# Gate and up tiles of the second feed-forward block: two tiles of eight K-tiles each as a 2x2x2 block product in seven multiplications

## The chip, the cores and the metric

The kernel runs on one core of a Trainium2 chip, as one launch. The metric is device time in microseconds (us); of the kernel before there are three runs, and their median counts. In the profile PE is TensorE's matmul, PEld its weight load, DVE is VectorE, ACT is ScalarE, POOL is GpSimd, and SP is the engine that issues the transfers.

## The reference

One layer of an encoder block for 512 tokens of width 1024, in float32: a half-step SwiGLU feed-forward block, a parallel token mixing (a sparse and a latent attention), and a second feed-forward block of the first one's form, then a last norm. The change is in the second feed-forward block:

```python
def swiglu(h, w_in, w_down):
    g, u = jnp.split(h @ w_in, 2, axis=-1)
    return (jax.nn.silu(g) * u) @ w_down
...
        h = modulate(rmsnorm(x, g_ffn2[l]), sh3, sc3)
        x = x + 0.5 * gt3[:, None, :] * swiglu(h, w_ffn2_in[l], w_ffn2_down[l])
    return rmsnorm(x, g_final)
```

w_ffn2_in is 1024 x 5632 (2816 gate columns, 2816 up columns), w_ffn2_down 2816 x 1024.

## The kernel before

Activations lie transposed, features on the 128 partitions and the 512 tokens along the free axis, so that weights are the stationary operand. A float32 operand is split on the chip into two float32r parts, hi and lo: ACT writes hi (a rounded copy), DVE or POOL writes lo = source - hi (`split`). A product is three matmuls into the same PSUM bank, hi*hi, hi*lo and lo*hi (`mm3`).

`swiglu` runs a feed-forward block. `first_group` makes the normalized and modulated input h K-tile by K-tile (8 K-tiles of 128 features, each with a hi and a lo part, `modulated`), and multiplies each at once, in halves of 256 tokens, with the weights of the first six output tiles: three gate and three up tiles. The other 19 gate tiles and 19 up tiles follow as pairs: for each pair two weight tiles of 512 KB are loaded and split (`weights`), and each is multiplied over the 8 K-tiles (`proj`) into a PSUM bank of its own. `gated` takes silu of the gate tile (ACT), multiplies it with the up tile (DVE, which reads PSUM), and splits the result into a hidden tile's two parts. The 22 hidden tiles come in thirds of 8, 7 and 7 (THIRDS); after each third, eight down tiles multiply its hidden tiles with w_ffn2_down and add to x. So pairs come in runs of 5, 7 and 7. In the last third the last four down tiles run in halves of 256 tokens, and each half's final norm follows as soon as it can.

The order of the work isn't written out. The block is traced into a list of operations (`Plan.record`), each with an estimated cost (`Plan.cost`), and a list scheduler (`Plan.order`) gives each engine its queue: of the operations that could start now, the one that was traced first. Each cost is estimated for the operation by itself. An operation starts when its operands are there and a buffer for its result is free. SBUF is 66 slots of 2 KB and 17 of 4 KB per partition (SLOTS); each kind of buffer has a limit (CAPS): one staging tile (wst), seven tiles each of weight parts (whi, wlo, 4 KB each). PSUM is eight banks, of which projections use six. The engines then work through their queues in order, and wait by semaphores where they must. All operations go through one recorded call, so every row of the profile has the line L602 of `issue`; rows are told apart by their tiles: f2h and f2l are the parts of h, wh_ and wl_ weight parts, ws_ staged weights, and of weight tiles _f is the first group's, _2g, _2u and _2d the gate, up and down tiles, hh and hl the hidden tiles' parts. Buffer numbers are left out.

POOL has no work in the second feed-forward block but clearing one half tile at its beginning.

Of the kernel before, what the change touches and what calls it, by code (L numbers as in the profile page):

```python
"""Hybrid streaming-encoder residual block: macaron SwiGLU, DSA + MLA token mixing, macaron SwiGLU.

Activations are kept transposed, features on the partitions and the 512 tokens along the free
axis, so that every projection has its weights stationary and streams N = 512 tokens. A float32
product runs as three passes of the tensor engine: each operand is split exactly into two
12-bit-significand parts (float32r) on the chip, and hi*hi + hi*lo + lo*hi accumulate in PSUM.
"""
# [17 lines left out]
P = 128  # L25
# [21 lines left out]
# the work up to the end of the first projections, in the order of its urgency, and what engines wait for  # L47
# [18 lines left out]
WG_POOL = (1, 3)  # L66
RING = 2
# [3 lines left out]
CAPS = {"x": 4, "x2": 8, "sq": 4, "h": 16, "hid": 20, "sg": 1, "mt0": 2, "mt256": 2, "nrm": 6, "wst": 1, "whi": 7, "wlo": 7,  # L71
# [5 lines left out]
# the mixing: I index scores, A sparse queries, L latents, U latent values, R rotary queries, P query and key  # L77
# pairs, S and W scores and values of a latent head, T top-k, G gates, D and E scores and values of four sparse heads
# [5 lines left out]
# its operations in the order of their urgency, and what engines wait for  # L84
# [29 lines left out]
TINY = {"norm": 16, "top1": 2, "top2": 2, "top3": 2, "mla": 24, "dsa": 24}  # L114
# [8 lines left out]
# columns of the packed per-feature vectors  # L123
V_BADA, V_G1, V_GM, V_G2, V_GF, V_GCQ, V_GCKV = 0, 72, 80, 88, 96, 104, 107
# constants and the T5 table in the same pack
# [3 lines left out]
def _mt(w):  # L129
    """(K, M) -> [M/128][128 partitions of K][K/128][128]"""  # L130
    k, m = w.shape
    return w.reshape(k // P, P, m // P, P).transpose(2, 1, 0, 3)


def _prep(inp):
# [45 lines left out]
    # rows that mask the first 64 queries of each block from its last 64 keys: queries, keys  # L181
# [12 lines left out]
# The block below is traced once into a list of operations on buffers without addresses. A list  # L194
# scheduler then orders them over the engines, each operation by its priority as soon as its operands
# and a slot for its result are there, and gives every buffer its slot; they are issued in that order.
# [5 lines left out]
class View:  # L202
# [31 lines left out]

    def bitcast(self, dt):
        return View(self.buf, self.chain + [("bitcast", dt)], self.p, self.off, self.dims, dt)
# [5 lines left out]
    def box(self):  # L242
        """partitions, columns, and the runs of columns where these have holes"""
# [11 lines left out]
    def real(self):  # L255
        ap = self.buf.base()
        for kind, *a in self.chain:
            if kind == "get":
                ap = ap[a[0]]
            elif kind == "bitcast":  # L260
                ap = ap.bitcast(a[0])
            else:
                ap = ap.rearrange(a[0], **a[1])
# [44 lines left out]
class Clock:  # L308
    """the tensor engine's clock: half as fast after a window in which it did little"""
# [21 lines left out]
# functions of ScalarE by the table that it loads for them  # L331
# [3 lines left out]
class Plan:  # L335
# [13 lines left out]
    # -- tracing  # L349
    @contextlib.contextmanager  # L350
    def after(self, op, everything=False):
        """loads, or all work, that is not to run ahead of an operation"""
# [10 lines left out]
    def record(self, eng, nc_engine, fn, args, kw):  # L363
# [14 lines left out]
        if op.eng == "pe":  # L378
            # the share of the time in which rows of the array work
# [16 lines left out]
        for v in outs:  # L396
# [9 lines left out]
            if eng == "pe":  # L406
                # a group's first matmul clears the flags of the whole bank: it comes after all matmuls
                # that were there before, and before all that follow; its last one after all of it
# [28 lines left out]
    def cost(eng, fn, outs, ins, kw, args):  # L437
        """an estimate, for the order alone"""
# [20 lines left out]
    # -- scheduling  # L459
    def order(self):  # L460
# [28 lines left out]
        while len(done) < len(self.ops):  # L489
            best = None  # L490
            for e, lst in ready.items():
# [4 lines left out]
                for op in lst:  # L496
# [4 lines left out]
                    for b in op.banks:  # L501
                        # a bank serves one engine at a time
# [9 lines left out]
                # an engine is not to begin something long just before urgent work  # L512
# [62 lines left out]
    def classes(b):  # L575
        """the kinds of slots that hold the buffer; a small one may take a large slot"""
        return (BANK,) if b.tag in BANK_CAPS else [c for c in SLOTS if c >= b.units]

    def take(self, b, live, s):
        """the slot that has been free for longest"""  # L580
# [24 lines left out]
class Block:  # L605
# [8 lines left out]
    def small(self, kind, n=4):  # L614
        """per-partition scalars, from a ring of its own for each kind of use"""
# [11 lines left out]
    def later(self):  # L627
        """work that only fills what the rest leaves free"""
# [5 lines left out]
    def urgent(self, *engines):  # L634
        """work that all of the next work waits for"""
# [4 lines left out]
    def split(self, hi, lo, src, engine=None):  # L640
        """hi + lo == src: hi rounded to float32r by ScalarE, the rest by VectorE"""
# [12 lines left out]
    def mm3(self, ps, wh, wl, xh, xl, start, stop, hh=True):  # L654
        mm = self.nc.tensor.matmul
        if hh:
            mm(ps, wh, xh, start=start, stop=False)
        mm(ps, wh, xl, start=False, stop=False)
        mm(ps, wl, xh, start=False, stop=stop)

    def proj(self, w, x, nk, name, tag, cols=ALL):
        """one tile of 128 output features: sum over nk K-tiles"""
# [8 lines left out]
    def squares(self, norm, t, cols=ALL, alone=False):  # L671
        """add a tile's squares to the sums of a norm, or keep them for the tensor engine to add"""
# [886 lines left out]
```

## Time and profile before

| | us |
|---|---|
| runs | 1180.87, 1183.2, 1185.97 |
| median of the runs | 1183.2 |
| span of the profiled execution, first to last instruction | 1182.4 |
| PE busy in it | 1137.4 |
| second block: from its first pair's first matmul to the last pair's end | 288.4 |

The page gives the profiled execution's span alone; what lies around it isn't told, so its own time is taken as the span. That lies within the three runs, 0.8 us below their median. In the profile, a row of a group gives its busy time, the mean of one in ns, and the idle time of its engine just before it with what ended it. Matmuls are pipelined: the record of one reaches over the beginning of the next, so the time that one costs is the distance of the starts.

### The profile page before, as it was taken

Reading aid. Unit: us, or ns where it says so; the run is one execution under the profiler, and the core shown is the slowest. Engines: PE = TensorE matmul, PEld = TensorE weight load, DVE = VectorE, ACT = ScalarE, POOL = GpSimd, SP = SyncE. Lnnn points to the kernel's source line nnn. Section 1 sums busy time; section 2 is a strip of 40 time slices with the busy share of each in tenths; the row PEclk is TensorE's granted clock in tenths of the full one; section 3 lists DMA queues with packets and bytes.
Section 4 is the critical chain, followed back from the end, with each engine's and each line's share of the span. In section 5 each row is a group of like instructions: output and inputs, shape, how many; then the busy total and the mean of one; then the engine's idle time right before and its main releaser. Section 6 shows DMA issues by size and latency. Waiting matters only on the chain. (4 is left out here: it accounts for less than half of the span.)

```text
span 1182.4 us, 15861 instructions
## 1 busy us (share of the span) xinstructions
PE 1137.4 (96%) x5955; PEld 949.1 (80%) x5957; DVE 744.1 (63%) x1381; ACT 502.6 (43%) x896; POOL 123.3 (10%) x111
## 2 busy tenths in 40 slices
PE   5999999999999999988999999999999999999996
PEld 3878788887877899776888777889988888888886
DVE  8876665547664796899997786848433333333335
ACT  5562413423343256454768777524432222223220
POOL 5120000000000000021235352000000000000000
PEclk8899999999999999999999999999999999999998
DMA  8555566548545753221144256423322332333212
GB/s 292 188 182 180 171 225 194 175 166 271 182 152 184 264 172 121 72 81 65 55 127 123 95 190 209 157 68 112 107 97 99 92 105 78 100 107 100 83 32 71
DMA packets 64543, 163.88 MB, mean 139 GB/s; under 512 B 9762, under 2 KB 21538, under 8 KB 64467
## 3 DMA queue, kind: packets, MB, share of 16 engines
q1 hardware_dynamic: 64466, 162.88, 41.7%
q8 instruction: 46, 0.75, 0.3%
q14 instruction: 31, 0.25, 0.1%
HBM read 148.11 MB, written 13.63 MB: 137 GB/s over the span
## 5 line engine op out<-in xcount | busy, mean ns | idle before, releaser
L602 DVE CUSTOM_DVE_ANT_0 junk<-ada,sc,vecs 128x1024 bf16<-128x1024 f32 x66 | 84.5, 1281 | 28.6 <-DMA ada<-in_w_ada_dram 28.4
L602 PE MATMUL bank<-hmh,wh_ib 128*128 128x512 f32 x200 | 79.8, 400 | 1.7 <-ACT wh_ib L602 1.7
L602 PE MATMUL bank<-hmh,wl_ib 128*128 128x512 f32 x200 | 80.2, 404 | 0.3 <-POOL wl_ib L602 0.3
L602 PE MATMUL bank<-hml,wh_ib 128*128 128x512 f32 x200 | 79.5, 398 | 0.0
L602 DVE TENSOR_TENSOR wl_2d<-ws_2d,wh_2d 128x896 fp32r<-128x896 f32 (+1 forms) x24 | 27.3, 1137 | 75.2 <-ACT wh_2d L602 75.2
L602 PE MATMUL bank<-hl,wh_2d 128*128 128x512 f32 (+1 forms) x204 | 73.6, 361 | 0.0
L602 PE MATMUL bank<-hh,wh_2d 128*128 128x512 f32 (+1 forms) x204 | 73.5, 360 | 0.0
L602 PE MATMUL bank<-hh,wl_2d 128*128 128x512 f32 (+1 forms) x204 | 73.4, 360 | 0.0
L602 PE MATMUL bank<-hh,wh_1d 128*128 128x512 f32 (+1 forms) x197 | 72.6, 369 | 0.0
L602 PE MATMUL bank<-hl,wh_1d 128*128 128x512 f32 (+1 forms) x197 | 72.4, 367 | 0.0
L602 PE MATMUL bank<-hh,wl_1d 128*128 128x512 f32 (+1 forms) x197 | 72.2, 366 | 0.0
L602 DVE TENSOR_TENSOR wl_2g<-ws_2g,wh_2g 128x1024 fp32r<-128x1024 f32 x19 | 23.3, 1225 | 60.1 <-ACT wh_2g L602 60.1
L602 DVE SCALAR_TENSOR_TENSOR x<-bank,gt,x 128x512 f32<-128x512 f32 (+1 forms) x66 | 44.0, 666 | 25.5 <-PE bank L602 25.4
L602 PE MATMUL bank<-f1h,wh_1g 128*128 128x512 f32 x152 | 59.5, 391 | 0.0
L602 PE MATMUL bank<-f1l,wh_1g 128*128 128x512 f32 x152 | 59.2, 389 | 0.0
L602 PE MATMUL bank<-f1h,wl_1g 128*128 128x512 f32 x152 | 59.2, 389 | 0.0
L602 PE MATMUL bank<-f2h,wh_2g 128*128 128x512 f32 x152 | 59.1, 389 | 0.0
L602 PE MATMUL bank<-f2l,wh_2g 128*128 128x512 f32 x152 | 59.1, 389 | 0.0
L602 PE MATMUL bank<-f1h,wh_1u 128*128 128x512 f32 x152 | 59.1, 389 | 0.0
L602 PE MATMUL bank<-f1l,wh_1u 128*128 128x512 f32 x152 | 59.1, 389 | 0.0
L602 PE MATMUL bank<-f2h,wl_2g 128*128 128x512 f32 x152 | 59.1, 389 | 0.0
L602 PE MATMUL bank<-f2h,wh_2u 128*128 128x512 f32 x152 | 59.1, 389 | 0.0
(328 smaller groups left out, 3088.2 us busy)
## 6 DMA issues: line engine op xcount, KB each, us to landing
ada<-in_w_ada_dram SPq DMA_DIRECT2D x72, 512.0 KB, 4.5
ws_ib<-in_wib_dram SPq DMA_DIRECT2D x25, 512.0 KB, 3.4
ws_1g<-in_w1b_dram SPq DMA_DIRECT2D x19, 512.0 KB, 3.7
ws_1u<-in_w1b_dram SPq DMA_DIRECT2D x19, 512.0 KB, 3.5
ws_2g<-in_w2b_dram SPq DMA_DIRECT2D x19, 512.0 KB, 3.7
ws_2u<-in_w2b_dram SPq DMA_DIRECT2D x19, 512.0 KB, 3.4
ws_1d<-in_w1d_dram SPq DMA_DIRECT2D x16, 448.0 KB, 3.5
ws_2d<-in_w2d_dram SPq DMA_DIRECT2D x16, 448.0 KB, 3.2
```

The source lines that it names most:

```text
L602: op.fn(*[real(v) for v in op.args], **{k: real(v) for k, v in op.kw.items()})
```

## The change

For a pair of a gate and an up tile, the K-tiles are taken in two halves (0 to 3, 4 to 7) and the tokens in two halves (a and b), so that the pair is a product of a 2x2 by a 2x2 matrix of blocks. It is made by seven block products in place of eight, each of 4 K-tiles and 256 tokens.

On the weights' side POOL makes four sums and differences of 128x512 per pair, and the parts of the staged gate tile (p0), of the combinations (p12, p34) and of half of the up tile (p22) are written; the lo part of p22 is POOL's. On the tokens' side four combinations are made for each of the four pairs of K-tiles k and k+4, once, in `token_combinations`; for that the modulated tiles are kept (m2), and `first_group` takes the K-tiles in the order 0, 4, 1, 5, 2, 6, 3, 7. In this group POOL writes the lo part of the weights of K-tiles 4, 5 and 6. On the output side the products accumulate in two PSUM banks, A and C: a product is added in PSUM to one whose value has been copied out before, and DVE adds the others, three times 256 columns and once 512. Loads of the pairs' weights wait for the matmuls of the third K-tile of the first group.

```diff
+W2_POOL = (4, 5, 6)
+FAST_FROM = 2
...
+CAPS = {"m2": 5, "fst": 3, "t2": 4, "th": 16, "wct": 3, "vhi": 2, "vlo": 2, "g4": 2, "sv": 2, "x": 4,
...
-    def modulated(self, h, x, r, a, sh, cols):
+    def modulated(self, h, x, r, a, sh, cols, kept=None):
         nc = self.nc
         hi, lo = (t[:, cols] for t in h)
-        t = self.g(f"m{h[0].name}_{cols.start}", shape=(P, cols.stop - cols.start), tag=f"mt{cols.start}")
+        t = kept[:, cols] if kept is not None else self.g(f"m{h[0].name}_{cols.start}", shape=(P, cols.stop - cols.start), tag=f"mt{cols.start}")
         nc.vector.scalar_tensor_tensor(t, x[:, cols], a, r[:, cols], op0=ALU.mult, op1=ALU.mult)
         nc.scalar.activation(hi, t, AF.Identity, bias=sh)
         nc.vector.scalar_tensor_tensor(lo, t, sh, hi.bitcast(F32), op0=ALU.add, op1=ALU.subtract)
 
-    def first_group(self, name, site, r, src, n, widths, before=None, w0=None):
+    def first_group(self, name, site, r, src, n, widths, before=None, w0=None, fast=None):
...
-        h = []
+        h = [None] * KD
...
-        for k in range(KD):
+        ks = [k // 2 + KD // 2 * (k % 2) for k in range(KD)] if fast is not None else list(range(KD))
+        kept = {}
+        for k in ks:
             with at(f"w{k}"):
                 wh, wl = w0 if w0 and not k else self.weights(
-                    src[k], f"{name}{k}", n, engine=nc.gpsimd if not site and k in W0_POOL else None)
+                    src[k], f"{name}{k}", n,
+                    engine=nc.gpsimd if not site and k in W0_POOL or fast is not None and k in W2_POOL else None)
             if before:
...
-            h.append(tuple(self.g(f"{name}{c}{k}", F32R, tag="h") for c in "hl"))
+            h[k] = tuple(self.g(f"{name}{c}{k}", F32R, tag="h") for c in "hl")
+            if fast is not None:
+                kept[k] = self.g(f"m{name}{k}", tag="m2")
...
                 with self.urgent() if k < URGENT else contextlib.nullcontext(), at(f"m{k}{i}"):
-                    self.modulated(h[k], self.x[k], r, a, sh, cols)
+                    self.modulated(h[k], self.x[k], r, a, sh, cols, kept.get(k))
                 with at(f"f{k}{i}"):
...
                         self.mm3(first[m][:w, cols], wh[:, c], wl[:, c], h[k][0][:, cols], h[k][1][:, cols],
-                                 False, k == KD - 1 and cols.stop == S, not start)
+                                 False, k == ks[-1] and cols.stop == S, not start)
+            if fast is not None and k == ks[FAST_FROM]:
+                self.fast_from = nc.last_pe
+            if fast is not None and k >= KD // 2:
+                fast.append(self.token_combinations(f"{name}t{k}", site, k - KD // 2, kept[k - KD // 2], kept[k]))
         return first, h
 
+    def token_combinations(self, name, site, k, m0, m1):
+        nc = self.nc
+        V = nc.vector
+        a, b = HALVES
+        sh = self.mod[:, site * 24 + k + KD // 2:site * 24 + k + KD // 2 + 1]
+        d = self.small("shift", 1)
+        V.tensor_tensor(d, sh, self.mod[:, site * 24 + k:site * 24 + k + 1], op=ALU.subtract)
+        t12, t34 = (self.g(f"{name}{i}", shape=(P, 2, S // 2), tag="t2") for i in (1, 3))
+        nc.gpsimd.tensor_tensor(t12[:, 0], m0[:, b], m0[:, a], op=ALU.subtract)
+        V.scalar_tensor_tensor(t34[:, 0], m1[:, b], d, m0[:, b], op0=ALU.add, op1=ALU.subtract)
+        V.scalar_tensor_tensor(t12[:, 1], m1[:, b], sh, t12[:, 0], op0=ALU.add, op1=ALU.subtract)
+        V.scalar_tensor_tensor(t34[:, 1], m1[:, a], sh, t12[:, 1], op0=ALU.add, op1=ALU.subtract)
+        out = []
+        for i, t in enumerate((t12, t34)):
+            hi, lo = (self.g(f"{name}{c}{i}", F32R, shape=(P, 2, S // 2), tag="th") for c in "hl")
+            self.split(hi, lo, t)
+            out += [(hi[:, e], lo[:, e]) for e in range(2)]
+        return out
+    def fast_pair(self, name, src0, src1, h, t):
+        nc = self.nc
+        V, G = nc.vector, nc.gpsimd
+        a, b = HALVES
+        half = S // 2
+        K4 = KD // 2
+        w0, w1 = (self.g(f"ws_{name}{i}", shape=(P, D), tag="fst") for i in range(2))
+        with nc.after(self.fast_from):
+            nc.sync.dma_start(w0, src0)
+            nc.sync.dma_start(w1, src1)
+        s12, s34 = (self.g(f"wc_{name}{i}", shape=(P, D), tag="wct") for i in range(2))
+        lo_, hi_ = slice(0, S), slice(S, D)
+        G.tensor_tensor(s12[:, hi_], w1[:, lo_], w1[:, hi_], op=ALU.add)
+        G.tensor_tensor(s12[:, lo_], s12[:, hi_], w0[:, lo_], op=ALU.subtract)
+        G.tensor_tensor(s34[:, lo_], w0[:, lo_], w1[:, lo_], op=ALU.subtract)
+        G.tensor_tensor(s34[:, hi_], w0[:, hi_], s12[:, lo_], op=ALU.subtract)
+        def parts(n, t, tag, w, engine=None):
+            hi = self.g(f"wh_{name}{n}", F32R, shape=(P, w), tag=tag + "hi")
+            lo = self.g(f"wl_{name}{n}", F32R, shape=(P, w), tag=tag + "lo")
+            self.split(hi, lo, t, engine)
+            return hi, lo
+        p0 = parts("a", w0, "w", D)
+        p12 = parts("s", s12, "w", D)
+        p34 = parts("t", s34, "w", D)
+        p22 = parts("b", w1[:, hi_], "v", S, G)
+        A, C = (self.bank(f"{n}_{name}", "mm") for n in "ac")
+        cols = lambda hs, at: [(hs[0][:, at + k * P:at + k * P + P], hs[1][:, at + k * P:at + k * P + P]) for k in range(K4)]
+        def product(ps, w, x, start=False):
+            for k in range(K4):
+                self.mm3(ps, *w[k], *x[k], start and k == 0, k == K4 - 1, skip_group_check=True)
+        quarter = lambda k0, c: [(h[k0 + k][0][:, c], h[k0 + k][1][:, c]) for k in range(K4)]
+        T = [[t[k][i] for k in range(K4)] for i in range(4)]
+        g = self.g(f"g_{name}", shape=(P, 4, half), tag="g4")
+        v = self.g(f"v_{name}", shape=(P, 2, half), tag="sv")
+        product(A[:, a], cols(p0, 0), quarter(0, a), True)
+        product(A[:, b], cols(p12, 0), T[1])
+        product(C[:, a], cols(p12, S), T[0], True)
+        product(C[:, b], cols(p34, 0), T[2])
+        nc.scalar.copy(v[:, 0], A[:, a])
+        V.tensor_tensor(v[:, 0], v[:, 0], A[:, b], op=ALU.add)
+        product(A[:, a], cols(p0, S), quarter(K4, a))
+        V.tensor_tensor(v[:, 1], v[:, 0], C[:, a], op=ALU.add)
+        V.tensor_tensor(g[:, 3], v[:, 1], C[:, b], op=ALU.add)
+        product(C[:, a], cols(p34, S), quarter(K4, b))
+        product(C[:, b], cols(p22, 0), T[3])
+        V.tensor_tensor(g[:, 1:3], v[:, 0].repeat(2), C.rearrange("p (e t) -> p e t", e=2), op=ALU.add)
+        return g, A[:, a]
...
     def swiglu(self, n, site, r, before_group=None, w0=None, fill=None, after_group=None):
         nc, A = self.nc, self.A
+        combos = [] if n == 2 else None
         first, h = self.first_group(f"f{n}", site, r, A[f"w{n}a"], 2 * FIRST * P, [P] * (2 * FIRST),
-                                    before_group, w0)
+                                    before_group, w0, combos)
         if after_group:
             after_group()
         hid = [None] * NP_FF
...
             gated(i, first[2 * i], first[2 * i + 1])
+        def gated_fast(i):
+            src = A[f"w{n}b"][i - FIRST]
+            g, c11 = self.fast_pair(f"f{i}", src[0], src[1], h, combos)
+            nc.scalar.activation(g[:, 0], c11, AF.Silu)
+            nc.scalar.activation(g[:, 1], g[:, 1], AF.Silu)
+            nc.vector.tensor_tensor(g[:, 0:2], g[:, 0:2], g[:, 2:4], op=ALU.mult)
+            hi, lo = self.g(f"hh{n}_{i}", F32R, tag="hid"), self.g(f"hl{n}_{i}", F32R, tag="hid")
+            e = lambda t: t.rearrange("p (e t) -> p e t", e=2)
+            nc.scalar.copy(e(hi), g[:, 0:2])
+            nc.vector.tensor_tensor(e(lo), g[:, 0:2], e(hi).bitcast(F32), op=ALU.subtract)
+            hid[i] = (hi, lo)
         for t, (i0, i1) in enumerate(THIRDS):
             for i in range(max(i0, FIRST), i1):
+                if n == 2:
+                    gated_fast(i)
+                    continue
                 pool = lambda e: nc.gpsimd if n == 1 and 2 * (i - FIRST) + e in WG_POOL else None
                 wg = self.weights(A[f"w{n}b"][i - FIRST, 0], f"{n}g{i}", engine=pool(0))
...
```

`View.repeat` makes a view that reads one tile twice; `mm3` hands `skip_group_check` on; comments and docstrings are left out of the new file.

## Rows read from the trace of the kernel before

**Rows 1.** The page: busy time of each engine, and POOL's tenths in 40 slices.

```profile
PE 1137.4 (96%) x5955; PEld 949.1 (80%) x5957; DVE 744.1 (63%) x1381; ACT 502.6 (43%) x896; POOL 123.3 (10%) x111
...
POOL 5120000000000000021235352000000000000000
```

**Rows 2.** Windows: length, busy us and instructions of PE, PEld, DVE, ACT, POOL; clock, DMA.

```profile
841.10:1129.50 288.40, 288.40 (x1275) 238.87 (x1274) 102.99 (x112) 80.62 (x97) 0.00 (x0) 1.00 0.29 95
797.00:841.00 44.00, 44.00 (x362) 43.60 (x361) 30.20 (x72) 19.51 (x31) 0.00 (x0) 1.00 0.36 111
```

**Rows 3.** Waits of PE from 805 to 1175 us: total, times, longest.

```profile
PE bank L602 <- DVE dg_n L602: 2.5, 1, 2.5
```

**Rows 4.** Timeline of PE, last pair: start us, duration us, operation.

```profile
1118.58 0.39 PE L602 MATMUL bank<-f2h,wh_2g 128*128 128x512 f32 x1
...
1124.02 0.39 PE L602 MATMUL bank<-f2h,wh_2u 128*128 128x512 f32 x1
...
1129.46 0.39 PE L602 MATMUL bank<-hh,wh_2d 128*128 128x512 f32 x1
```

**Rows 5.** Timeline of PE, last down tiles in halves: first matmul of each half.

```profile
1148.50 0.28 PE L602 MATMUL bank<-hh,wh_2d 128*128 128x256 f32 x1
...
1158.57 0.28 PE L602 MATMUL bank<-hh,wh_2d 128*128 128x256 f32 x1
```

**Rows 6.** Windows, within those halves.

```profile
1149.00:1160.00 11.00, 11.00 (x94) 11.00 (x93) 4.62 (x10) 2.30 (x5) 0.00 (x0) 1.00 0.01 1
```

**Rows 7.** Timelines, POOL (two rows) and DVE (two rows): starts of operations in succession.

```profile
702.03 1.29 POOL L602 TENSOR_TENSOR bt<-bt,mask 128x512 f32<-128x512 f32 x1
703.28 0.45 POOL L602 TENSOR_TENSOR oal<-osA,oah 64x128 fp32r<-64x128 f32 x1
...
822.45 1.22 DVE L602 TENSOR_TENSOR wl_2g<-ws_2g,wh_2g 128x1024 fp32r<-128x1024 f32 x1
823.58 0.88 DVE L602 SCALAR_TENSOR_TENSOR f2l<-mf2h,mod,f2h 128x256 fp32r<-128x256 f32 x2
```

**Rows 8.** Groups of DVE by shape: busy us, mean ns, idle before.

```profile
L602 DVE TENSOR_TENSOR hl<-sg,hh 128x512 fp32r<-128x512 f32 x44 | 30.4, 691 | 22.4 <-ACT hh L602 22.4
...
L602 DVE TENSOR_TENSOR wl_2g<-ws_2g,wh_2g 128x1024 fp32r<-128x1024 f32 x19 | 23.3, 1225 | 60.1 <-ACT wh_2g L602 60.1
...
L602 DVE SCALAR_TENSOR_TENSOR f2l<-mf2h,mod,f2h 128x256 fp32r<-128x256 f32 x16 | 7.3, 482 | 1.6 <-ACT f2h L602 1.6
...
L602 DVE TENSOR_TENSOR acc_n<-acc_n,sq_n 128x256 f32<-128x256 f32 x17 | 7.3, 427 | 2.6 <-ACT sq_n L602 2.3
```

**Rows 9.** Groups of ACT by shape.

```profile
L602 ACT CAST wh_2g<-ws_2g 128x1024 fp32r<-128x1024 f32 x19 | 19.9, 1050 | 57.0 <-DMA ws_2g<-in_w2b_dram 57.0
```

**Rows 10.** Timelines, DVE and POOL side by side: two meetings.

```profile
57.73 0.75 DVE L602 SCALAR_TENSOR_TENSOR f1l<-mf1h,mod,f1h 128x512 fp32r<-128x512 f32 x1
58.39 0.74 DVE L602 SCALAR_TENSOR_TENSOR mf1h<-x,a,bank 128x512 f32<-128x512 f32 x1
57.84 2.88 POOL L602 TENSOR_TENSOR adap<-ada,sc 128x1024 f32<-128x1024 f32 x1 [4.72 <-DVE wl_f L602]
...
503.43 0.69 DVE L602 TENSOR_TENSOR cql<-lat,cqh 128x512 fp32r<-128x512 f32 x1
504.43 2.49 DVE L602 TENSOR_TENSOR cql<-lat,cqh 128x512 fp32r<-128x512 f32 x1
504.00 2.38 POOL L602 TENSOR_TENSOR wl_ib<-ws_ib,wh_ib 128x1024 fp32r<-128x1024 f32 x1 [8.69 <-ACT wh_ib L602]
```

**Rows 11.** Timeline of DVE, first group: the second half's norm arrives.

```profile
814.21 0.87 DVE L602 SCALAR_TENSOR_TENSOR mf2h<-x,a,bank 128x256 f32<-128x256 f32 x2 [0.59 <-PE bank L602]
```

**Rows 12.** Groups of POOL by shape.

```profile
L602 POOL TENSOR_TENSOR bt<-bt,mask 128x256 f32<-128x256 f32 x8 | 6.4, 804 | 6.2 <-DVE osB L602 5.2 <-DVE mask L602 0.6 <-DMA bt<-bias 0.4
...
L602 POOL TENSOR_TENSOR wl_f<-ws_f,wh_f 128x768 fp32r<-128x768 f32 x2 | 4.3, 2128 | 13.1 <-DVE mod L602 7.9 <-ACT wh_f L602 5.2
```

More of the change, by code (lines that the diff above doesn't have):

```diff
@@ L70 @@
 SLOTS = {1: 66, 2: 17}
-CAPS = {"x": 4, "x2": 8, "sq": 4, "h": 16, "hid": 20, "sg": 1, "mt0": 2, "mt256": 2, "nrm": 6, "wst": 1, "whi": 7, "wlo": 7,
+CAPS = {"m2": 5, "fst": 3, "t2": 4, "th": 16, "wct": 3, "vhi": 2, "vlo": 2, "g4": 2, "sv": 2, "x": 4, "x2": 8, "sq": 4, "h": 16, "hid": 20, "sg": 1, "mt0": 2, "mt256": 2, "nrm": 6, "wst": 1, "whi": 7, "wlo": 7,
         "ust": 2, "uhi": 3, "ulo": 2, "ada": 3, "junk": 1, "adap": 2, "zero": 1, "dn": 1, "mr": 1, "sc": 2, "t5m": 8, "t5o": 2, "t5i": 2, "t5d": 1,
@@ L113 @@
 """
-TINY = {"norm": 16, "top1": 2, "top2": 2, "top3": 2, "mla": 24, "dsa": 24}
+TINY = {"norm": 16, "shift": 4, "top1": 2, "top2": 2, "top3": 2, "mla": 24, "dsa": 24}
 BANK_CAPS = {"mm": 6, "rn": 2, "t5": 2, "ix": 2, "mg": 3, "uk": 1, "sa": 3, "sb": 3, "tpa": 2, "tpb": 1,
@@ L233, in rearrange, with repeat @@
         return View(self.buf, self.chain + [("rearrange", pat, kw)], self.p, self.off, dims, self.dt)
+    def repeat(self, n):
+        return View(self.buf, self.chain + [("repeat", n)], self.p, self.off, [(0, n)] + self.dims, self.dt)
     def bitcast(self, dt):
@@ L261, in real @@
                 ap = ap.bitcast(a[0])
+            elif kind == "repeat":
+                ap = ap.unsqueeze(1)
+                ap = ap.broadcast_to([ap.shape[0], a[0], *ap.shape[2:]])
             else:
@@ L652, in weights, with mm3 @@
         return hi, lo
-    def mm3(self, ps, wh, wl, xh, xl, start, stop, hh=True):
+    def mm3(self, ps, wh, wl, xh, xl, start, stop, hh=True, **kw):
         mm = self.nc.tensor.matmul
         if hh:
-            mm(ps, wh, xh, start=start, stop=False)
-        mm(ps, wh, xl, start=False, stop=False)
-        mm(ps, wl, xh, start=False, stop=stop)
+            mm(ps, wh, xh, start=start, stop=False, **kw)
+        mm(ps, wh, xl, start=False, stop=False, **kw)
+        mm(ps, wl, xh, start=False, stop=stop, **kw)
     def proj(self, w, x, nk, name, tag, cols=ALL):
```

## The prediction, made before the changed kernel ran

> **What bounds the kernel now.** I read the page's shares first: TensorE (PE) is busy for 1137.4 of 1182.4 us, GpSimd (POOL) for 10% of it, and by the slices POOL does next to nothing in the last 40% of the span [rows 1]. Then the table by stage: in the second feed-forward block's 288.4 us of gate, up and down tiles PE is busy without a gap at granted clock 1.00 (the 2.4 GHz level), VectorE (DVE) for 103.0 and ScalarE (ACT) for 80.6 us, POOL for nothing, and the DMA share is 0.29 [rows 2]. Last, PE's waits from 805 us to the end: the longest is 2.5 us, on the last norm, outside that stretch [rows 3]. So here PE sets the time alone: 19 pairs of gate and up tiles, and 16 of the 24 down tiles. A microsecond of matmul taken out counts in full, as long as the others keep feeding PE.
>
> **Matmuls.** A pair is 2 tiles x 8 K-tiles x 3 passes = 48 matmuls of 512 tokens; from 1118.58 to 1129.46 they took 10.88 us, 226.7 ns each [rows 4]. 19 pairs are 206.7 us. The change makes of a pair 7 products x 4 K-tiles x 3 passes = 84 matmuls of 256 tokens. The trace holds this form: the first halves of the last four down tiles are 4 x 7 x 3 = 84 such matmuls with a new weight each, and took 1158.57 - 1148.50 = 10.07 us, 119.9 ns each [rows 5]. It is not the 7/8 that the columns promise, since 2 x 119.9 is 6% over 226.7; the weight loads are busy for 11.00 of 11.00 us there [rows 6]. Per pair 0.81 us goes, over 19 pairs **15.4 us**. Both terms come from the same shapes, so I give them no width.
>
> A rule of the Trainium skill speaks against this: "TensorE: Matmul & The Clock Gate", section The mechanism, has a weight load overlap a running matmul only when their row groups differ, and these fill all rows. With that page's load time of 107 ns and its 107 ns for 256 columns a matmul would take about 214 ns (an estimate from that page) and a pair 18 us. The 119.9 ns of rows 5, for the same form, decide against it.
>
> **First group.** Its 288 matmuls stay, only the K order changes (0, 4, 1, 5, ...). I cost that at nothing: PE is busy through 797 to 841 us [rows 2], and DVE, at 30.2 of 44.0 us, is the cover; what DVE gets in addition is in the next part.
>
> **What feeds the pairs.** Per pair POOL gets five 128x512 operations with two SBUF inputs (four weight combinations, one lo part). One takes 1.25 us from start to start [rows 7], so 6.25 us. DVE gets three lo parts of 128x1024 instead of two (record 1.225 us [rows 8]; records overlap the next by 0.09 [rows 7], so 1.13), the gate product and the hidden lo part (0.60 each), and four additions that read PSUM (3 x 0.34 + 0.60): 3.39 + 1.20 + 1.62 = 6.2 us. ACT gets three 1.05 us conversions [rows 9] and about 2.4 us of smaller work: 5.6 us. Taken singly, all lie under PE's 10.07. Loads stay two of 512 KB per pair.
>
> Taken together they don't, and this is the part that decides. DVE operations with two SBUF inputs and POOL operations don't run side by side here: a DVE subtraction of 128x512 began at 504.43 and took 2.49 us where it needs 0.69, and ended 0.54 after the POOL operation of 504.00 to 506.38; a POOL operation beginning at 57.84 took 2.88 instead of some 2.4 behind a DVE operation; a DVE operation with a PSUM input, at 58.39, ran in its usual 0.74 beside it [rows 10]. The pair's shared claim is POOL 6.25 + DVE 3.39 + 1.20 = **10.84 us**, against 10.07 for PE. What carries it is that the pairs come in runs of 5, 7 and 7, with eight down tiles between, in which POOL has nothing to do and DVE one lo part per tile. The 17 large slots hold a pair's six weight parts and the next pair's staging and combinations, so I count one pair prepared ahead of the second and of the third run, worth about 10 us, against a shortage of 7 x 0.77 = 5.4 us. Those two runs should keep PE fed on the average.
>
> The first run has no such lead. From 814.2, where the second half's norm reaches DVE [rows 11], to the end of the fifth pair (841.1 + 5 x 10.07 = 891.5) there are 77.3 us, and the shared claim is: 8 lo parts of h at 0.39, 3.1; token combinations, 4 x (3 x 0.39 + 2 x 0.60 + POOL 0.80 [rows 12]), 12.7; the last two of the first group's weights, one on each engine (0.86 + 2.1 [rows 12]), 3.0; five pairs' preparation at 9.64, 48.2; gates, 13 x 0.60, 7.8. That is 74.8 of 77.3, leaving no room for an unlucky order. I take **3 us** lost; the bounds are 0 (a perfect order) and 8 (the shared port idle for a tenth of that time).
>
> **The new handoffs.** No matmul waits for DVE inside a pair now. The fifth product accumulates over a bank half that ACT and DVE must have copied, the sixth over one that DVE must have added (two additions, 0.68 us plus the signals, under the fifth product's 12 x 0.12 = 1.44 us). So some 0.4 us is to spare, and it goes when DVE, which works in order, stands behind POOL with a lo part. Queued behind that lo part are the additions, and PE behind these; ACT's copy can likewise stand behind a conversion whose combination is late. POOL holds the port for 62% of a pair with 0.63 us left on average, and about half the time such a DVE operation is in front: 0.62 x 0.63 x 0.5 = 0.2. I take 0.25 per pair, **4.8 us**; bounds 0 and 1.25 (one whole POOL operation) per pair, 24 us. At the ends of the runs the gate is 0.6 us longer, covered by the seven K-tiles that the next down tile can start with. The order is planned ahead from single costs that take no account of this, so an inversion stays in it.
>
> **Sum.** 1182.4 - 15.4 + 3 + 4.8 = 1174.8 us of span. The median of the three runs is 0.8 above the span of the profiled execution, so **1176 us**. A measurement of this kernel can tell 0.5%, 5.9 us, from no change.
>
> **Rivals.**
> 1. *The port never shows.* Prefetch and slack hide all of it: 1182.4 - 15.4 + 0.8 = 1168. For it: DVE has 3.9 us per pair free, and PE's real 119.9 ns gives all others time. Against it: 97% of the port in the first run. Chance 0.20.
> 2. *The port sets the pairs' pace.* Then each of 17 pairs (two being prepared ahead) takes 10.84: 17 x 10.84 + 2 x 10.07 = 204.4 against 206.7; 1181. That is no change, and the saved multiplications would be paid for with additions. For it: the claim exceeds PE's need. Against it: the down tiles' gaps. Chance 0.20. "Perfetto Trace Analysis" of the Trainium skill, section Optimizing Scalar/DVE Operations, warns that moving work between the two engines that share a port might not help; by that rule this rival is the outcome, and rows 10 agree on the blocking.
> 3. *Slower: DVE's order stands in line too.* Where the PSUM additions don't run under POOL but wait behind blocked lo parts, DVE's 1.62 us adds to the 10.84: up to 12.46 per pair. It decides from 10.98 upward, the pace at which 17 pairs eat the whole gain; beyond 11.3 it is slower by 0.5%. Midway, 11.65: 17 x 11.65 + 20.1 = 218.2, which is 11.5 more than now, 1195; at the top 1208. For it: one queue, in order, with PE at the end of it. Against it: a lo part that was let through frees the additions just while POOL has the port. Chance 0.18.
>
> **How the numbers follow.** The forecast has 0.42, with 1170 to 1181 as its own range; two thirds of it lie below 1177.3, where 0.5% begins. Faster 0.20 + 0.28 = 0.48; same 0.14 + 0.20 = 0.34; slower 0.18. The range reaches from the case without loss, less what runs differ by, to the middle of rival 3: 1167 to 1194.
>
> **What would show it.** A pair's 84 matmuls in 10.07 us where PE isn't interrupted; POOL near 6.25 us per pair; DVE lo parts with records of 2 us and more beside POOL; PE waits that name DVE or ACT at the fifth and sixth products, most of them in the first run. Pairs at 10.07 throughout mean rival 1; an even pace near 10.8 with PE waiting for weight parts, rival 2; an even pace over 11 with PE waiting for the additions, rival 3. The sum is wrong from the bottom if 256-token matmuls come at more than 120 ns, or if the granted clock leaves 1.00 in the pairs.

## The result, and the profile after

The changed kernel took 1216.0 us (median of four, 1214.5 to 1222.5) against 1182.8 for the kernel before in the same job: a ratio of 1.029 (1.025 to 1.032), slower. Forecast was 1176, with a range of 1167 to 1194: wrong in sign and outside the range. The profiled execution has a span of 1214.9 us, 32.5 more than before's.

The page, part 1 and two rows of slices [rows 1]:

```profile
PE 1137.0 (94%) x6641; PEld 976.0 (80%) x6641; DVE 866.7 (71%) x1497; ACT 543.3 (45%) x980; POOL 302.7 (25%) x213
...
POOL 5120000000000000220353540017470378137500
```

PE is busy as long as before, though it now has fewer columns to stream (in the same version with GpSimd left out of it, further down, it is busy for 1122.0 us). POOL works in three bursts, the three runs of pairs. By the timeline the first pair begins at 844.3 instead of 841.1 us, and the stage to the last pair's end takes 320.5 us instead of 288.4; the end is 2.8 us shorter. Windows, with the columns of [rows 2]. The first line is the first group and the second is the first run of pairs; the others are cut roughly, since the second run goes from 957.5 to 1041.9 us and the third from 1079.6 to 1164.8, with down tiles between them:

```profile
797.00:841.00 44.00, 42.81 (x348) 42.12 (x348) 39.69 (x84) 19.30 (x35) 15.86 (x12) 1.00 0.32 99
841.00:913.00 72.00, 58.44 (x443) 56.41 (x442) 57.68 (x56) 30.74 (x47) 45.09 (x26) 0.93 0.28 87
913.00:963.00 50.00, 50.00 (x248) 42.50 (x248) 23.48 (x24) 14.29 (x16) 5.83 (x4) 1.00 0.27 86
963.00:1050.00 87.00, 77.34 (x582) 72.68 (x581) 63.67 (x63) 33.41 (x54) 58.92 (x33) 1.00 0.30 94
1050.00:1090.00 40.00, 40.00 (x219) 34.91 (x218) 17.90 (x20) 11.71 (x13) 7.63 (x5) 1.00 0.24 75
1090.00:1170.00 80.00, 71.79 (x539) 68.79 (x539) 58.84 (x63) 33.97 (x52) 42.35 (x23) 0.98 0.28 87
```

PE stands idle only where pairs run, never over down tiles, and in the first run the granted clock is 0.93. No other engine is full there: DVE is busy for 57.7 of 72 and 63.7 of 87 us, POOL for 45.1 and 58.9. What PE waits for, from 795 to 1215 us [rows 3]:

```profile
PE bank L611 <- DVE g_f L611: 13.1, 13, 3.1
PE bank L611 <- DVE v_f L611: 12.9, 12, 5.4
PE bank L611 <- DVE dg_n L611: 3.7, 2, 2.5
PE bank L611 <- ACT v_f L611: 3.3, 5, 1.5
```

Without dg_n these are the new handoffs, 29.3 us of them: the copy and the additions that a pair's matmuls stand behind. By PE's timeline they stop the fifth product twice, the sixth thirteen times, the seventh ten times (for g_f), and the second five times (for ACT's copy out of the bank that it writes). The first run took 69.5 us for five pairs (844.3 to 913.8), the others 84.4 and 85.1 us for seven: 13.9, 12.1 and 12.2 us a pair instead of 10.07 (the third run has 13 matmuls of down tiles among its own, 2.9 us). How a handoff comes late is seen in a stretch of the second run: DVE, then POOL, ACT and PE (start us, us, operation, and in brackets the idle time before it with what ended it):

```profile
986.75 1.78 DVE L611 TENSOR_TENSOR hl<-g_f,hh 128x512 fp32r<-128x512 f32 x1
988.45 0.41 DVE L611 TENSOR_TENSOR v_f<-v_f,bank 128x256 f32<-128x256 f32 x1
988.78 1.96 DVE L611 TENSOR_TENSOR wl_f11t<-wc_f,wh_f11t 128x1024 fp32r<-128x1024 f32 x1
990.67 2.32 DVE L611 TENSOR_TENSOR wl_f12a<-ws_f,wh_f12a 128x1024 fp32r<-128x1024 f32 x1
992.91 0.41 DVE L611 TENSOR_TENSOR g_f<-v_f,bank 128x256 f32<-128x256 f32 x1
...
988.06 1.60 POOL L611 TENSOR_TENSOR wc_f<-wc_f,ws_f 128x512 f32<-128x512 f32 x1
989.63 2.28 POOL L611 TENSOR_TENSOR wc_f<-ws_f,ws_f 128x512 f32<-128x512 f32 x1
991.87 2.25 POOL L611 TENSOR_TENSOR wc_f<-ws_f,wc_f 128x512 f32<-128x512 f32 x1
...
994.16 1.05 ACT L611 CAST wh_f12t<-wc_f 128x1024 fp32r<-128x1024 f32 x1 [2.27 <-POOL wc_f L611]
995.11 0.36 ACT L611 COPY v_f<-bank 128x256 f32<-128x256 f32 x1
...
992.37 0.28 PE L611 MATMUL bank<-f2t5l,wh_f11s 128*128 128x256 f32 x1
993.37 0.39 PE L611 MATMUL bank<-f2t4h,wh_f10b 128*128 128x256 f32 x1 [0.72 <-DVE g_f L611]
993.60 0.28 PE L611 MATMUL bank<-f2t4l,wh_f10b 128*128 128x256 f32 x1
...
995.53 0.38 PE L611 MATMUL bank<-f2t5h,wl_f11s 128*128 128x256 f32 x1 [0.45 <-ACT v_f L611]
```

Low parts that need 1.22 us alone take 1.96 and 2.32 beside POOL [rows 8], and POOL's 1.25 [rows 7] become 2.28: strict turns, as at the meetings of [rows 10]. Behind two such low parts, both for later pairs, stands the 0.41 us addition that PE waits for; on ACT the copy stands behind a conversion that waited 2.27 us for a combination. The additions themselves, with a PSUM operand, are not stretched (0.41 us).

A stop costs PE more than the list says. The matmul at 993.37 starts 1.00 us after the one before it and the next one 0.23 us later, where 0.12 is usual: 0.99 us are lost for 0.72 listed. Over the 31 stops in the three runs the list has 31.2 us (the 29.3, and 1.9 for a low part of the token combinations), and 8.4 us come on top.

### The profile page after: what moved, and what is told of

Its sections match the earlier page's. It is cut to its first block, busy times and chain, and to the rows that moved or that the text cites. A ratio compares the mean times of both kernels' runs of the same rounds, so it can differ in the third digit from the quotient of the medians.

```text
span 1214.9 us, 17623 instructions
## 1 busy us (share of the span) xinstructions
PE 1137.0 (94%) x6641; PEld 976.0 (80%) x6641; DVE 866.7 (71%) x1497; ACT 543.3 (45%) x980; POOL 302.7 (25%) x213
## 5 line engine op out<-in xcount | busy, mean ns | idle before, releaser
L611 POOL TENSOR_TENSOR wl_ib<-ws_ib,wh_ib 128x1024 fp32r<-128x1024 f32 x16 | 39.0, 2436 | 134.2 <-ACT wh_ib L611 99.3
L611 PE MATMUL bank<-f1h,wl_1u 128*128 128x512 f32 x152 | 59.2, 389 | 0.0
L611 POOL TENSOR_TENSOR wc_f<-ws_f,ws_f 128x512 f32<-128x512 f32 x19 | 37.0, 1946 | 76.7 <-PE bank L611 76.7
L611 DVE TENSOR_TENSOR wl_1d<-ws_1d,wh_1d 128x896 fp32r<-128x896 f32 (+1 forms) x24 | 27.3, 1137 | 39.0 <-ACT wh_1d L611 27.3
L611 ACT CAST wh_1d<-ws_1d 128x896 fp32r<-128x896 f32 (+1 forms) x24 | 23.5, 978 | 63.5 <-DMA ws_1d<-in_w1d_dram 56.0
```

The source lines that it names most:

```text
L611: op.fn(*[real(v) for v in op.args], **{k: real(v) for k, v in op.kw.items()})
```

## The experiments

Theory A held that the meeting of POOL and DVE is the source and the in-order queues carry it to PE. Its rivals: B, the handoffs alone; C, too few staging buffers and slots; later P, the shared port's own pace; and D, the order that the planner writes. Where no range is given, a version ran once; seven runs of the kernel before lay between 1181.0 and 1189.2 us.

**All weight combinations on VectorE.**

```diff
-        G.tensor_tensor(s12[:, hi_], w1[:, lo_], w1[:, hi_], op=ALU.add)
+        V.tensor_tensor(s12[:, hi_], w1[:, lo_], w1[:, hi_], op=ALU.add)
...
-        p22 = parts("b", w1[:, hi_], "v", S, G)
+        p22 = parts("b", w1[:, hi_], "v", S)
```

> The changed kernel with the four weight combinations of a pair and the low parts of w22 on VectorE instead of GpSimd. Theory A (GpSimd and VectorE take turns at shared memory, and VectorE's in-order queue carries that to the products that wait for its additions): VectorE then has about 10.5 us of work per pair (three 128x1024 low parts at 1.22, four combinations and a low part at 0.69, additions, gate and low part of the hidden tile some 3.4), close to TensorE's 10.07, so 1172 to 1195 us, with the 128x1024 low parts back at about 1.23 us. Rival B (the new handoffs inside a pair cost this by themselves, whoever makes the weights): 1210 to 1222. Rival C (too few staging buffers and large slots set the pace): 1205 to 1220.

Measured: 1172.7 us (1168.8 to 1173.5), ratio to before 0.991 (0.989 to 0.993). PE's waits from 795 us on:

```profile
PE bank L611 <- DVE dg_n L611: 3.6, 2, 2.5
PE bank L611 <- ACT sq_n L611: 1.0, 1, 1.0
```

Every handoff is still there and none is late; starts of pairs in the second run are 10.0 to 10.1 us apart (962.2, 972.3, 982.3, 992.4). DVE had room for it, though not much: in the second run (934.8 to 1006.7 us) it is busy for 62.9 of 71.9 us; in the changed kernel's second run it was busy for 61.1 of 84.6, the combinations being POOL's. B falls, and C with it, since the buffers and their limits are the same.

**No combinations at all.**

```diff
-        s12, s34 = (self.g(f"wc_{name}{i}", shape=(P, D), tag="wct") for i in range(2))
+        s12, s34 = w1, w0
...
-        G.tensor_tensor(s12[:, hi_], w1[:, lo_], w1[:, hi_], op=ALU.add)
```

> The changed kernel without the four weight combinations: w1 and w0 are split in place of the combined tiles, so the products are not Strassen's. GpSimd keeps the low parts of w22 and the first stretch. Theory A: VectorE about 7.7 us per pair, GpSimd 1.3, nothing left to take turns with: pairs at about 10.1 to 10.5 us, 1166 to 1182 us. Rival B (handoffs by themselves): 1205 to 1220. Rival C (slots and staging): three large slots fewer per pair are needed, so it expects a gain as well, 1175 to 1195.

Measured: 1171.1 us. Beside this, the combinations on VectorE cost nothing that shows (1172.7), and on GpSimd they cost 45 us.

**No waits inside a pair.**

```diff
         product(C[:, b], cols(p34, 0), T[2])
+        product(A[:, a], cols(p0, S), quarter(K4, a))
+        product(C[:, a], cols(p34, S), quarter(K4, b))
+        product(C[:, b], cols(p22, 0), T[3])
         nc.scalar.copy(v[:, 0], A[:, a])
         V.tensor_tensor(v[:, 0], v[:, 0], A[:, b], op=ALU.add)
-        product(A[:, a], cols(p0, S), quarter(K4, a))
         V.tensor_tensor(v[:, 1], v[:, 0], C[:, a], op=ALU.add)
         V.tensor_tensor(g[:, 3], v[:, 1], C[:, b], op=ALU.add)
-        product(C[:, a], cols(p34, S), quarter(K4, b))
-        product(C[:, b], cols(p22, 0), T[3])
```

> The changed kernel with the copy and the additions of v and g moved behind the seventh product: the same operations on the same engines, but no product of a pair waits for them (the values are not those of the scheme). Theory A: the combinations on GpSimd still set the pace, so TensorE's waits move from the additions to the weights: 1195 to 1215 us. Rival B: the handoffs were the whole loss, 1166 to 1180 us. Rival C: as A, 1200 to 1216.

Measured: 1193.1 us, 23 less than the changed kernel and outside all three ranges, though the meeting goes on: POOL's combinations take 1.59 to 1.89 us on the average of a group, and the pairs' 128x1024 low parts 1.73 us on the average of 57, as in the changed kernel (1.22 without the meeting). Starts of pairs are 10.1 us apart in the second and third run (956.7, 966.8, 976.9, 987.0). Against A, the meeting with GpSimd does not set the pace: TensorE's waits moved not to the weights of the pairs but mostly to the hidden tiles at the three ends of the runs:

```profile
PE bank L611 <- ACT hh L611: 10.1, 3, 4.0
PE bank L611 <- DVE dg_n L611: 3.6, 2, 2.5
PE bank L611 <- DVE f2t7l L611: 1.9, 1, 1.9
PE bank L611 <- DVE wl_f6s L611: 1.7, 1, 1.7
```

Of the 20 us over the version of the first experiment, these ends hold 10.1 and the first run 6.2 (56.5 us instead of 50.3).

**The meeting in the kernel before.**

```diff
                 pu = self.proj(wu, h, KD, f"pu{n}_{i}", "mm")
+                if n == 2:
+                    for q in range(5):
+                        w = (wg, wu)[q // 3][0].bitcast(F32)
+                        z = self.g(f"z{i}_{q}", tag="sv")
+                        nc.gpsimd.tensor_tensor(z, w[:, 0:S], w[:, S:D], op=ALU.add)
```

> The kernel before with five GpSimd additions of 128x512 per pair in the second block, whose results nobody reads: the meeting of GpSimd and VectorE without the new handoffs. Theory A: VectorE's 128x1024 low parts rise from 1.23 to about 2 us in these stretches, GpSimd's additions take 1.8 to 2.2; a pair's VectorE work becomes some 7 us and stays under TensorE's 10.88, so the time is 1182 to 1190 us. If the meeting alone were enough, without any handoff, over 1200. Rival B and C: 1181 to 1185, with the low parts little changed.

Measured: 1182.5 us beside 1183.8 for the kernel before: no change. The groups of the second block by shape, DVE's and POOL's:

```profile
L602 DVE TENSOR_TENSOR wl_2u<-ws_2u,wh_2u 128x1024 fp32r<-128x1024 f32 x16 | 24.7, 1545 | 31.6 <-ACT wh_2u L602 27.9 <-POOL z L602 3.6
L602 DVE TENSOR_TENSOR wl_2g<-ws_2g,wh_2g 128x1024 fp32r<-128x1024 f32 x16 | 22.8, 1428 | 49.6 <-ACT wh_2g L602 49.6
...
L602 POOL TENSOR_TENSOR z<-wh_2u 128x512 f32<-128x512 f32 x38 | 67.1, 1786 | 3.2 <-ACT wh_2u L602 2.9
```

The low parts went from 1.22 us to 1.43 and 1.55 (less than the 2 expected) and PE did not wait once for a pair: there, weights only have to be ready before a tile begins. By itself, with nothing that PE waits for inside a pair, the meeting cost nothing in this kernel.

**Half of the combinations on GpSimd.**

```diff
-        G.tensor_tensor(s12[:, hi_], w1[:, lo_], w1[:, hi_], op=ALU.add)
-        G.tensor_tensor(s12[:, lo_], s12[:, hi_], w0[:, lo_], op=ALU.subtract)
+        V.tensor_tensor(s12[:, hi_], w1[:, lo_], w1[:, hi_], op=ALU.add)
+        V.tensor_tensor(s12[:, lo_], s12[:, hi_], w0[:, lo_], op=ALU.subtract)
```

> Two of the four weight combinations of a pair (those of the second combined tile) stay on GpSimd, the other two and the low parts of w22 go to VectorE. Theory A (what is lost are the waits of TensorE for the additions inside a pair, which stand in VectorE's in-order queue behind low parts that take turns with GpSimd; with no such waits nothing is lost): a dose too small to make TensorE wait costs nothing, 1168 to 1182 us, low parts at 1.5 to 1.9 us on average. Rival P (the shared port itself sets the pace, each us on it counts): in proportion to GpSimd's operations, 2 of 5 of the 43 us between all on VectorE and the changed kernel, 1186 to 1194. Rival C (slots and staging): as the kernel with all combinations on VectorE, 1170 to 1176.

Measured: 1181.8 us, with 5.7 us of waits for v and g left. The price is below what P asks (1186) and at the upper end for A: a small dose is not free. Taken alone it decides little.

**The planner's costs set to the trace.** The operations are those of the changed kernel.

```diff
+        if outs[0].buf.name.startswith("wc_f"):
+            return 1900.0
+        if eng == "dve" and outs[0].buf.tag == "wlo" and outs[0].buf.name[-1] in "ast" and outs[0].buf.name[:4] == "wl_f":
+            return 2000.0
         if eng == "pool":
```

> The changed kernel, with the planner's costs set to what the trace shows: 1.9 us for a combination on GpSimd (it had 1.23) and 2.0 us for a 128x1024 low part of a pair on VectorE (it had 1.14). Only the order and the slots change. Rival D (the order, planned with prices that leave out the meeting, is the whole loss): 1168 to 1185 us. Theory A: the additions come further ahead in VectorE's queue, but each low part still holds it for 2.3 us, so a part is won back: 1185 to 1207. Rival P (port sets the pace): 1207 to 1220, no change.

Measured: 1181.4 us: 35 us back by two numbers, which change the order and the slots. The meeting goes on nearly as it was: low parts take 1.61 us on the average of 57 (1.73 in the changed kernel), and two POOL groups are:

```profile
L615 POOL TENSOR_TENSOR wc_f<-ws_f,wc_f 128x512 f32<-128x512 f32 x19 | 37.0, 1945 | 0.3
L615 POOL TENSOR_TENSOR wc_f<-wc_f,ws_f 128x512 f32<-128x512 f32 x19 | 34.3, 1807 | 0.7
```

and the waits of PE from 795 us on are nearly gone:

```profile
PE bank L615 <- DVE dg_n L615: 3.7, 2, 2.5
PE bank L615 <- DVE g_f L615: 2.5, 4, 1.1
PE bank L615 <- ACT v_f L615: 1.3, 1, 1.3
PE bank L615 <- DVE f2t7l L615: 1.2, 1, 1.2
```

In DVE's timeline the addition of g now stands ahead of both low parts that it stood behind, or, in the next pair, of one of the two:

```profile
971.75 0.41 DVE L615 TENSOR_TENSOR v_f<-v_f,bank 128x256 f32<-128x256 f32 x1
972.27 0.42 DVE L615 TENSOR_TENSOR g_f<-v_f,bank 128x256 f32<-128x256 f32 x1
972.61 1.47 DVE L615 TENSOR_TENSOR wl_f11t<-wc_f,wh_f11t 128x1024 fp32r<-128x1024 f32 x1
...
974.59 1.21 DVE L615 TENSOR_TENSOR wl_f12a<-ws_f,wh_f12a 128x1024 fp32r<-128x1024 f32 x1
...
981.87 1.52 DVE L615 TENSOR_TENSOR wl_f12t<-wc_f,wh_f12t 128x1024 fp32r<-128x1024 f32 x1 [0.38 <-ACT hh L615]
...
985.01 0.41 DVE L615 TENSOR_TENSOR g_f<-v_f,bank 128x256 f32<-128x256 f32 x1
985.35 1.99 DVE L615 TENSOR_TENSOR wl_f13a<-ws_f,wh_f13a 128x1024 fp32r<-128x1024 f32 x1
```

P falls: nearly the same meeting, and pairs 10.1 us apart (951.5, 961.6, 971.6, 981.7). A's idea that each stretched low part still holds the queue falls as well (1185 to 1207 expected).

**Each cost alone**, the first or the second condition of that diff.

> Of the two planner costs that gave 1181.4 us together, only GpSimd's: 1.9 us for a combination. Theory D (the loss is an order planned at prices that leave the meeting out, on any engine): a part is won back, 1185 to 1205 us, more than with VectorE's price alone if the late start of the combinations is what the plan had wrong. If VectorE's queue (where a low part stands ahead of an addition) is what the plan had wrong: over 1205.

> Only VectorE's: 2.0 us for a 128x1024 low part of a pair. If what the plan had wrong is VectorE's queue, most is won back: 1181 to 1192 us. If it is GpSimd's pace: 1200 to 1216.

Measured: 1191.1 us with POOL's, 1192.8 with DVE's (just over the 1192 of its range). Each wins back some two thirds, so neither cost alone is at fault; over 1205 was expected with POOL's alone if only VectorE's queue had been planned wrongly.

**Urgent additions.**

```diff
-        nc.scalar.copy(v[:, 0], A[:, a])
-        V.tensor_tensor(v[:, 0], v[:, 0], A[:, b], op=ALU.add)
+        with self.urgent("act", "dve"):
+            nc.scalar.copy(v[:, 0], A[:, a])
+            V.tensor_tensor(v[:, 0], v[:, 0], A[:, b], op=ALU.add)
```

(and the same for the two additions behind the fifth product.)

> The changed kernel with the copy and the three additions that products wait for marked urgent, so that the planner begins nothing long on VectorE or ScalarE just before one. Theory A: waits for the additions fall from 29 us to 10 to 20, 1192 to 1208 us. Rival D (order alone): 1168 to 1185. Rival P: 1207 to 1220.

Measured: 1205.8 us, with 22.0 us of waits for v and g left. The planner decides by planned times what is urgent in time; I take it that this is why it helped so little here.

**Right costs, and the first stretch on VectorE.** To the diff of the costs:

```diff
-W2_POOL = (4, 5, 6)
+W2_POOL = ()
...
-        nc.gpsimd.tensor_tensor(t12[:, 0], m0[:, b], m0[:, a], op=ALU.subtract)
+        V.tensor_tensor(t12[:, 0], m0[:, b], m0[:, a], op=ALU.subtract)
```

> Both planner costs, and the first stretch's work (three low parts, four token differences) on VectorE; the four combinations and the low parts of w22 stay on GpSimd. Theory D: the meeting goes on, low parts at 1.6 us on average and combinations at 1.7 to 1.95, and costs little where the order allows for it: 1172 to 1182 us, the first pair some 3 us earlier. If GpSimd's work in the first stretch cost nothing: 1180 to 1184.

Measured: 1180.1 us (1175.2 to 1183.9), ratio to before 0.996 (0.994 to 0.998). The first pair did not begin earlier (845.5 us, 845.3 without it), so the few us expected there did not come.

**GpSimd out of the change altogether**: both diffs, that of the first experiment and this last one, with the planner's costs as they were.

> As the kernel with all weight combinations on VectorE, and the first stretch's work too (three low parts and four token differences), so that the change uses GpSimd for nothing. Theory A: GpSimd meets nobody in the block; VectorE gets some 4.5 us more before the first pair, where it was busy 40 of 44 us, so 1167 to 1178 us, within 4 us of that kernel. If VectorE's load before the first pair decides, up to 1182.

Measured: 1170.1 us (1169.2 to 1173.3), ratio to before 0.988 (0.985 to 0.990), the lowest median, better than both kernels, though not clear of the version with only the weight combinations on VectorE (1172.7). In its stage PE is busy to the end; two windows:

```profile
841.00:913.00 72.00, 71.63 (x512) 67.41 (x511) 58.27 (x85) 32.84 (x49) 0.00 (x0) 1.00 0.38 117
963.00:1050.00 87.00, 87.00 (x578) 80.42 (x577) 60.91 (x86) 33.35 (x48) 0.00 (x0) 1.00 0.34 106
```

**Wrong costs without the meeting**: that kernel, with the two conditions of the costs returning 300.0 and 570.0.

> The kernel with GpSimd out of the change (1170.1 us), planned at half of VectorE's costs: 0.30 us for a combination that takes 0.69, 0.57 us for a low part that takes 1.22. No meeting, wrong prices. If wrong prices in the plan are enough for the loss: TensorE waits for additions of v and g again, 1182 to 1210 us. If the loss needs the meeting as well: 1168 to 1176.

Measured: 1187.8 us, and PE waits for the additions again:

```profile
PE bank L615 <- DVE g_f L615: 7.3, 11, 1.3
PE bank L615 <- DVE v_f L615: 2.7, 5, 1.0
```

An order planned for operations half as long as they are is enough for a loss of 18 us, with no GpSimd in it.

**The old order without the meeting.**

```diff
+            if op.eng == "pool" and op.args[0].buf.name.startswith("wc_f"):
+                self.real_gpsimd.memset(real(op.args[0]), 0.0)
+                continue
             op.fn(*[real(v) for v in op.args], **{k: real(v) for k, v in op.kw.items()})
```

> The changed kernel's own plan, order and slots, with the four weight combinations issued as GpSimd memsets of the same tiles (the combinations are left out, the tiles hold zeros), so that nearly all of the meeting is gone and the order is what it was. If that order is bad by itself, whatever the durations: 1190 to 1212 us, waits for v and g as in the changed kernel. If the loss is the mismatch between the order and the durations (an order planned for short operations, run with operations stretched by the meeting): 1168 to 1180, low parts at 1.23 us and no waits of TensorE inside the pairs.

Measured: 1170.3 us. The very order and slots that took 1216.0 leave no wait inside a pair once the meeting is gone: low parts take 1.23 us on the average. GpSimd's part of a combination also shrinks, to 0.53 us where the planner had 1.23, and needs no loaded weights, so this run takes out the length of the combinations along with the stretch of the low parts and can't tell the two apart. A pair of DVE's timeline, and two clearings by POOL:

```profile
971.06 1.23 DVE L614 TENSOR_TENSOR wl_f12s<-wc_f,wh_f12s 128x1024 fp32r<-128x1024 f32 x1 [0.30 <-PE bank L614]
972.20 0.69 DVE L614 TENSOR_TENSOR hl<-g_f,hh 128x512 fp32r<-128x512 f32 x1
972.80 0.41 DVE L614 TENSOR_TENSOR v_f<-v_f,bank 128x256 f32<-128x256 f32 x1
973.13 1.22 DVE L614 TENSOR_TENSOR wl_f12t<-wc_f,wh_f12t 128x1024 fp32r<-128x1024 f32 x1
975.31 1.23 DVE L614 TENSOR_TENSOR wl_f13a<-ws_f,wh_f13a 128x1024 fp32r<-128x1024 f32 x1 [0.95 <-PE bank L614]
976.45 0.42 DVE L614 TENSOR_TENSOR g_f<-v_f,bank 128x256 f32<-128x256 f32 x1
...
971.13 0.99 POOL L612 MEMSET wc_f<- 128x512 f32 x2 [1.36 <-PE bank L614]
```

It is the order of the stretch at 986 us above: hidden low part, addition, two low parts for later pairs, addition. Here both additions end before PE asks for them.

So four cases, in us:

| | the planner's own costs | costs from the trace |
|---|---|---|
| GpSimd and VectorE meet | 1216.0 | 1181.4 |
| they don't meet | 1170.3 | 1170.1 (GpSimd out, where the planner's own costs are about right) |

Most of the loss is neither the meeting alone nor the order alone but the mismatch of the two: an order fixed ahead, for durations that the meeting then stretches, with TensorE waiting inside the pairs for what stands last in a queue. Of the 46 us between 1216.0 and 1170.1, 35 go with the order and slots planned at the costs from the trace; the other 11 are taken up below.

## Why the prediction was wrong

- **Matmuls, 15.4 us: right.** Pairs took 10.0 to 10.1 us wherever PE wasn't held, and the version without GpSimd is 14.5 us under the kernel before of its job (1184.6). The weight loads cost nothing more. A rule of the Trainium skill, "TensorE: Matmul & The Clock Gate", section The mechanism, by which they would not have overlapped, is at odds with these 10.0 to 10.1 us; the same section also lets a load that goes to the background weight buffer run ahead, and with that they agree.
- **First group at nothing: right for the group, not for what it leaves behind.** In the changed kernel the first pair begins 3.2 us later than before, but 3.1 of these were there when the group began (807.55 us, 804.49 before): the group itself took 36.8 us instead of 36.6. The group began anywhere from 802.9 to 808.7 us in the kernels that were run. But the combinations of the first pairs fall into this stretch (POOL 15.9 us busy from 797 to 841 us, 5.5 with the weight combinations on VectorE), and PE then waits 1.9 us, inside the first pair, for the last low part of the token combinations.
- **What feeds the pairs: right as a sum, and not what decided.** Turns at the port came as told, and additions from PSUM ran beside POOL. The claim of 10.84 us did not set a pace, as held in the prediction: with the meeting kept, pairs came 10.1 us apart once the order allowed for it. That kernel's 11 us over the version without GpSimd are not all the meeting's: 4.4 were there when the first group began (808.50 and 804.12 us), and 7.4 more went in the three runs (4.3, 1.7 and 1.5). The sign of POOL near 6.25 us per pair did not come: stretched by the turns, the records of its five operations add up to 8.9. The Trainium skill, "Perfetto Trace Analysis", section Optimizing Scalar/DVE Operations, warns that shifting work between the two engines of one port might not help: the four combinations and one low part made by GpSimd against the same by VectorE, 1216.0 against 1172.7 us, agree, though by way of the order and not of the port's pace.
- **The first run, 3 us with a bound of 8: wrong.** It took 69.5 us instead of 50.4. The longest stop, 5.4 us for v in the first pair, was less DVE's than ACT's: the copy of v began at 858.40 us, behind three conversions and a table load of 1.28 us, and DVE stood 3.0 us for the first group's gate. Besides the stops, the clock fell: after PE had stood 1.9 us, and again after these 5.4, the granted clock was 0.50 (the 1.2 GHz level; 850 to 852 and 860 to 863 us), and 31 matmuls came 0.21 instead of 0.12 us apart, 2.9 us in all. In the third run, after a stop of 3.1 us, 15 more cost 1.4.
- **The handoffs, 0.25 us per pair: this is the step that failed.** I took POOL's share of the port times half an operation times one chance in two, as if a late addition stood behind a random piece of one operation. It stood behind one or two whole stretched low parts (of weights or of a hidden tile), pair after pair, since the same order repeats. And I had named the fifth and sixth products; the seventh and the second wait too. Against 4.8 us forecast, with a bound of 24, the runs showed 29.3 us of listed waits and 8.1 more around them, some 37 us. The second and third run lost 1.9 and 1.7 us a pair, down-tile matmuls taken out, beyond my bound of 1.25. Whether the loss also fed on itself, PE's lateness letting POOL begin late, is not shown: POOL waited 99.6 us for slots that PE still held, and 102.4 us with the costs from the trace. Of "an inversion stays in it" I had the mechanism in a sentence and gave it no price.
- **Rival 3: right in its sign, its waits and its mechanism, wrong in its price.** Its pace of 11.65 to 12.46 is where the two later runs fell (12.1 and 12.2), with the additions behind blocked low parts and PE behind the additions, as it said. But it priced this as work that adds up, 10.84 and 1.62 us per pair, and there its nearness is luck: with the costs from the trace the same operations ran at 10.1 us a pair. The whole came out above even its top, 1208, by the first run. It had 0.18, and the range ended at its middle: that was too little for the one case in which PE, an in-order queue and a stretched operation meet.
- **The sum.** Against 10.07 us a pair the three runs took 48.0 us more, and the rows add up to it: 29.3 us of handoffs, 1.9 for the token combinations' low part, 8.4 around these 31 stops, 4.3 by the lower clock, 0.7 for two stops that the list doesn't have, and 3.4 for the 15 matmuls of down tiles that ran among the pairs, which are no loss. My terms for these runs were 3 and 4.8.

## What to carry to other kernels

When a change puts a wait of the bounding engine behind an in-order queue, ask what stands ahead of it there, and how long that takes with everything else running, not alone. A static order is worth as much as the durations it was planned with: move work to an engine that slows its neighbour, and the costs of both have to move too (here 35 us for two numbers), or the work had better stay on one engine if that has the room, as VectorE had here. An average share of a port prices a pace; it does not price a position in a queue.

## What was not expected of the hardware

A GpSimd memset of 128x512 does not take turns with VectorE: two of them took 0.99 us from 971.13 on, while VectorE's low part from 971.06 kept its 1.23 us. An addition with two SBUF inputs of the same shape took 1.6 to 2.3 us in its place and stretched the low part to as much as 2.34. And in the meeting even a small operation pays for a whole turn: the hidden low part of 128x512 went from 0.69 to 1.78 us at 986.75.
